# Splits of the first and last unit issued in another order, and gate weights moved behind the turned blocks

## The chip, the cores and the metric

One program runs on one core of a Trainium2 chip. TensorE (PE) multiplies matrices and loads its stationary operand separately (PEld), VectorE (DVE), ScalarE (ACT) and GpSimd (POOL) work on SBUF, and SyncE (SP) and POOL issue DMAs. Each engine takes its instructions in order; between engines semaphores hold an instruction back until what it reads is there. The metric is the device time of the program in microseconds (us). Before the change it is 651.31 us, the median of 3 runs (650.48 to 651.41).

## The reference

A decoder trunk of two layers over 256 tokens and a model width D = 1024. Layer 0 mixes tokens with forgetting attention, layer 1 with block-sparse attention; the change touches neither mixer. Behind the mixer each layer has a gated FFN and a gated per-layer input (PLE), and a final norm ends the program:

```python
u = _rmsnorm(h, ffn_norm_g[i])
gu = u @ ffn_w_in[i]
h = h + (jax.nn.silu(gu[..., :D_FF]) * gu[..., D_FF:]) @ ffn_w_out[i]
gate = jax.nn.sigmoid(_rmsnorm(h, ple_norm_g[i]) @ ple_w_gate[i])
h = h + gate * (p[i] @ ple_w_up[i])
```

`x` is 1 x 256 x 1024, `D_FF` 2816, everything float32.

## The kernel before

**Precision.** Every float32 operand is split in a rounded high part (ACT copies it into a rounded type, fp32r in the profile) and a low remainder (DVE subtracts), and every product is three PE products: high by high, high by low, low by high (lines 96, 97 and 98 of `mm3`). So weights arrive in halves of 512 KB (`half`, by SP's queue into `raw`, 6 buffers), ACT makes `whi` (L158), DVE makes `wlo` (L159), each in a ring of 6 buffers. The weight halves of a layer are numbered in the order of use; the numbers in `whi82` or `wlo169` are theirs.

**FFN.** 22 blocks f of the hidden width are computed one after the other (`gu`, `up`), two of them make a unit u = 0 to 10 (NU = 11). `gated(f)` takes a block's result from PSUM: ACT makes `sg` (L676, L677), DVE multiplies into `a32` (L685). When the second block of a unit is there, DVE makes four sums of its parts (L691 to L693), and `halves(u)` splits all seven parts into `ah` (ACT, L619) and `al` (DVE, L620). The output product is done by a scheme with seven products instead of eight, so the weights of a unit are summed too: `unit(u)` fetches them (`xr<-wu` on POOL's DMA queue; SP's for the last unit), splits the first and the fourth quarter pair, makes sums on DVE (L643, L645, L648) and splits these (`uh`, `ul`; for the last unit they live in the weight ring and are called `whiu`, `wlou`). PE then runs `fo<-uh,ah` and so on (L658). A unit's products stand between later blocks' `gu` products (`visit`). The products of the last two units come after the last block, in an order written out by hand (`last`), and their accumulators are added to the residual h (L746).

**The turn to the PLE.** `Norm.turn` transposes a half of h on PE (`tp`, L212, four blocks per half), and `Norm.block` scales and splits it into `g` (ACT L202, DVE L203). The gate's first two weight halves are not split the usual way. `summed` fetches the half with rounding as `hi` through POOL's queue (L186), ACT writes its negative into `lo` (L187), and a second DMA of POOL adds the exact weights onto that (L188). The call for both of them stands behind the rounding of the last unit's last activations.

**PLE.** `ple` computes the gate in two halves of the width. The first half `pg_0` uses the two `summed` halves and two ordinary ones; after two weight halves the second half of h is turned (`nm.turn(1)`), squares (L226) give the norm's scale on DVE (L234, L235) and POOL (`col`, L237), and ACT loads the table for the sigmoid (L108). `gate` then applies sigmoid (ACT, `pgt`, L801), the product with the input (DVE, L802) and the addition to h (DVE, L803). The second half `pg_1` takes four more weight halves: 82 to 85 in layer 0, 168 to 171 in layer 1. In layer 0 the next layer's norm turns its first blocks among them; in layer 1 the second token half is computed last and in two narrow parts (`pg_1_1` and `pgl`, 256 wide), so that the final norm's work on ACT and DVE (`sqf`, `msf`, `end`, L837 to L890) lies beside PE.

**What sets the order.** The program is traced in Python, and a scheduler places instructions on each engine by its own estimate of when they can run. Three hints bind it: `tc.issue_after(x)` keeps what is inside behind x in its engine's order, `tc.keep_in_program_order` fixes the order as traced, and tile pools make a new tile wait for the last reader of the tile whose buffer it takes. `nm.behind()` is `issue_after` both instructions of the norm's last turned block.

Of the kernel before, what the change touches and what calls it, by code (L numbers as in the profile page):

```python
# [30 lines left out]
ALU = mybir.AluOpType  # L31

P = 128
# [42 lines left out]
def trunk(ctx: ExitStack, tc: tile.TileContext, x, xg, wx, xr, pt, w, wu, cst, gf, rel, hot, rvm, out):  # L76
# [12 lines left out]
    def f32(ap):  # L89
        return ap.bitcast(F32)  # L90
# [90 lines left out]
    def summed():  # L181

        i = state["next"]
        state["next"] += 1
        hi, lo = (work.tile([P, HW + 2 * LINE], F32R, tag=n, bufs=6, name=f"{n}{i}")[:, 0:HW] for n in ("whi", "wlo"))
        nc.gpsimd.dma_start(hi, w[i - 2][:, 0:HW])  # L186
        nc.scalar.activation(lo, f32(hi), AF.Copy, scale=-1.0)  # L187
        nc.gpsimd.dma_start(lo, w[i - 2][:, 0:HW], accum_op=ALU.add)  # L188
        return hi, lo
# [421 lines left out]
    def ffn(layer, nm):  # L611
# [4 lines left out]
        left, right = {}, {}  # L616
# [5 lines left out]
        def unit(u):  # L622
# [9 lines left out]
            def pair(n, wide=HW):  # L632
                if u == NU - 1 and n != 3:
# [3 lines left out]
                        for t in ("uh", "ul")]  # L637

            p0 = pair(0)
            splits(*p0, r1[:, 0:HW])  # L640
            p3 = pair(3, HC)
            splits(*p3, r2[:, HC:HW])
            nc.vector.tensor_tensor(xs[:, 0:2], r2[:, 0:HC].unsqueeze(1).to_broadcast([P, 2, HC]),  # L643
                                    r1[:, 0:HW].rearrange("p (a c) -> p a c", c=HC), op=ALU.add)
            nc.vector.tensor_tensor(xs[:, 2], xs[:, 0], r1[:, HC:HW], op=ALU.add)  # L645
            p1 = pair(1)
            splits(*p1, xs[:, 0:2].rearrange("p a c -> p (a c)"))
            nc.vector.tensor_tensor(xs[:, 3], xs[:, 2], r2[:, HC:HW], op=ALU.add)  # L648
            p2 = pair(2)
            splits(*p2, xs[:, 2:4].rearrange("p a c -> p (a c)"))  # L650
# [22 lines left out]
        def gated(f, bk):  # L673
# [8 lines left out]
            if f % 2 == 0 and u:  # L682
                with tc.issue_after(empty.ins):
                    halves(u - 1)
# [8 lines left out]
            nc.vector.tensor_tensor(a[:, 6], a[:, 1], a[:, 5], op=ALU.add)  # L693
            if u == NU - 1:
                halves(u, (3, 7))

# [8 lines left out]
        def up(fs):  # L705
# [17 lines left out]
            for f in fs:  # L723
                gated(f, bks[f])
# [9 lines left out]
        for u in (NU - 2, NU - 1):  # L734
            unit(u)
        rounded, split = left["end"]
        with tc.issue_after(rounded.ins):
            gate = [summed(), summed()]
# [57 lines left out]
    def ple(layer, nm, ut, nx, early):  # L796
# [19 lines left out]
        if layer == 0:  # L816
            for c in range(4):
                pair_unit(bks[1], c, half(), nm.k)
                if c == 2:
                    nx.turn(0)  # L820
                    nx.square(0)
            for t in range(2):
                gate(bks[1][t], t, HC, D)
            return
# [19 lines left out]
        wts = [half(AHEAD) for _ in range(4)]  # L844
# [164 lines left out]
```

## Time and profile before

| | us |
|---|---|
| median of 3 runs | 651.31 |
| profiled execution, its own time | 649.11 |
| span of that execution's profile | 647.3 |
| PE busy | 636.0 (98%) |
| DVE busy | 522.3 (81%) |
| ACT busy | 420.6 (65%) |

The granted TensorE clock was 0.998 over the span. The profile's rows give the start of an instruction, its length, the engine, the line, the operation and the tiles as out<-in, and in brackets the engine's idle time before it with what ended it. Instructions of one line that follow each other closely stand in one row (x2). PE's rows overlap, since products are pipelined; what tells of a wait there is the step from one start to the next.

### The profile page before, as it was taken

The numbers are of one execution on the slowest core, as the hardware profiler recorded it, in microseconds if no ns is written. First come the engines' busy times: TensorE is split into PE (matmuls) and PEld (weight loads), VectorE is DVE, ScalarE is ACT, GpSimd is POOL, SyncE is SP. The second block draws the span as 40 slices with busy tenths as digits, with TensorE's granted clock in tenths as the row PEclk, the third lists the DMA queues.
The fourth block names the chain that finished last, engine by engine and source line by source line (L and its number), as shares of the span: only waits on it lengthen the run. The fifth ranks groups of instructions, "written<-read, shape, count | busy, mean of one in ns | idle before, by whom it ended". The sixth has DMA issues, their size and how long they took to land.

```text
span 647.3 us, 11656 instructions
## 1 busy us (share of the span) xinstructions
PE 636.0 (98%) x4514; PEld 578.6 (89%) x4514; DVE 522.3 (81%) x824; ACT 420.6 (65%) x725; POOL 41.1 (6%) x75
## 2 busy tenths in 40 slices
PE   9999999999999999999999999999999999999995
PEld 7899987999999999997889999789999999999774
DVE  5778884779998888878875787658898888887886
ACT  6866774976666666547866677757666666665483
POOL 1000000200000000001100000010000000000111
PEclk9999999999999999999999999999999999999999
DMA  8978544568766666534896554445677666662711
GB/s 336 376 244 282 190 128 155 166 199 286 246 199 199 199 201 205 187 121 102 277 330 207 175 173 136 133 142 186 204 266 224 226 212 200 194 214 87 174 22 65
DMA packets 36599, 127.31 MB, mean 197 GB/s; under 512 B 3968, under 2 KB 6336, under 8 KB 36544
## 3 DMA queue, kind: packets, MB, share of 16 engines
q1 hardware_dynamic: 29216, 101.00, 47.5%
q0 software_dynamic: 6912, 25.17, 13.3%
q8 instruction: 35, 0.57, 0.3%
q10 hardware_dynamic: 416, 0.40, 0.2%
q14 instruction: 20, 0.16, 0.1%
HBM read 125.48 MB, written 4.22 MB: 200 GB/s over the span
## 4 chain that ended last, share of the span: by engine, by line
PE 87%; DMA 4%; issue 3%; DVE 2%; ACT 1%; POOL 1%; POOLq 0%; ACTq 0%; DVEq 0%
PE fo L658 15%; PE gu L97 11%; PE gu L96 10%; PE gu L98 10%; PE pq L96 5%; PE pq L97 5%; PE pq L98 5%; DMA xr<-wu 3%; PE wo L96 2%; PE wo L98 2%; PE wo L97 2%; PE v L98 2%; PE v L96 2%; PE v L97 2%; PE pg L96 2%
## 5 line engine op out<-in xcount | busy, mean ns | idle before, releaser
L96 PE MATMUL gu<-g,whi 128*128 128x256 f32 x704 | 195.1, 277 | 0.0
L98 PE MATMUL gu<-g,wlo 128*128 128x256 f32 x704 | 195.0, 277 | 0.0
L97 PE MATMUL gu<-g,whi 128*128 128x256 f32 x704 | 195.0, 277 | 0.0
L159 DVE TENSOR_TENSOR wlo<-raw,whi 128x1024 fp32r<-128x1024 f32 (+1 forms) x119 | 143.6, 1213 | 45.1 <-ACT whi L158 43.4
L158 ACT ACTIVATE whi<-raw 128x1024 fp32r<-128x1024 f32 (+1 forms) x118 | 122.9, 1055 | 79.4 <-PE gu L97 37.2
L97 PEld LDWEIGHTS gu<-g,whi 128*128 128x128 f32 x704 | 132.2, 188 | 1.6
L96 PEld LDWEIGHTS gu<-g,whi 128*128 128x128 f32 x704 | 132.2, 188 | 1.4
L98 PEld LDWEIGHTS gu<-g,wlo 128*128 128x128 f32 x704 | 132.3, 188 | 0.2 <-DVE wlo L159 0.2
L175 ACT ACTIVATE whi<-raw 128x1080 fp32r<-128x1080 f32 x47 | 52.0, 1107 | 56.9 <-PE gu L97 47.3
L620 DVE TENSOR_TENSOR ul<-xr,uh 128x1024 fp32r<-128x1024 f32 (+1 forms) x80 | 85.8, 1088 | 1.9 <-ACT uh L619 1.9
L619 ACT ACTIVATE uh<-xr 128x1024 fp32r<-128x1024 f32 (+1 forms) x80 | 73.4, 953 | 10.6 <-DMA xr<-wu 9.1
L176 DVE TENSOR_TENSOR wlo<-raw,whi 128x1080 fp32r<-128x1080 f32 x47 | 60.2, 1281 | 14.5 <-ACT whi L175 14.5
L96 PE MATMUL pq<-g,whi 128*128 128x256 f32 x256 | 71.7, 280 | 0.0
L97 PE MATMUL pq<-g,whi 128*128 128x256 f32 x256 | 71.0, 277 | 0.0
L98 PE MATMUL pq<-g,wlo 128*128 128x256 f32 x256 | 71.0, 277 | 0.0
L658 PE MATMUL fo<-uh,al 128*128 128x512 f32 x142 | 55.7, 392 | 0.5 <-DVE al L620 0.5
L658 PE MATMUL fo<-uh,ah 128*128 128x512 f32 x142 | 55.7, 393 | 0.0
L658 PE MATMUL fo<-ul,ah 128*128 128x512 f32 x142 | 55.5, 391 | 0.0
L96 PEld LDWEIGHTS pq<-g,whi 128*128 128x128 f32 x256 | 48.3, 189 | 1.1 <-issue 0.6
L97 PEld LDWEIGHTS pq<-g,whi 128*128 128x128 f32 x256 | 48.1, 188 | 0.0
L98 PEld LDWEIGHTS pq<-g,wlo 128*128 128x128 f32 x256 | 48.1, 188 | 0.0
L630 POOL DMA_DIRECT2D xr<-wu x40 | 21.7, 543 | 263.5 <-DVE ul L620 195.3
(196 smaller groups left out, 1097.3 us busy)
## 6 DMA issues: line engine op xcount, KB each, us to landing
raw<-w SPq DMA_DIRECT2D x118, 512.0 KB, 4.6
raw<-w SPq DMA_DIRECT2D x47, 540.0 KB, 4.5
xr<-wu POOLq DMA_DIRECT2D x40, 512.0 KB, 5.9
d<-d SPq DMA_DIRECT2D x4, 768.0 KB, 9.4
ru<-wu SPq DMA_DIRECT2D x4, 512.0 KB, 5.2
whi<-w POOLq DMA_DIRECT2D x4, 512.0 KB, 3.7
wlo<-w POOLq DMA_DIRECT2D x4, 512.0 KB, 6.4
bias<-d SPq DMA_DIRECT2D x4, 512.0 KB, 5.4
```

Source lines behind the costliest of these rows:

```text
L96: mm(o, ah, bh, start=start, stop=False, skip_group_check=True)
L97: mm(o, ah, bl, start=False, stop=False, skip_group_check=True)
L98: mm(o, al, bh, start=False, stop=stop, skip_group_check=True)
L158: nc.scalar.activation(hi[:, c], raw[:, c], AF.Copy)
L159: nc.vector.tensor_tensor(lo[:, c], raw[:, c], f32(hi[:, c]), op=ALU.subtract)
L175: nc.scalar.activation(ht, raw[:, 0:WW], AF.Copy)
L176: nc.vector.tensor_tensor(lt, raw[:, 0:WW], f32(ht), op=ALU.subtract)
L619: first = nc.scalar.activation(hi, src, AF.Copy)
L620: return first, nc.vector.tensor_tensor(lo, src, f32(hi), op=ALU.subtract)
L630: queue.dma_start(r, wu[layer * NU + u][:, i * HW:(i + 1) * HW])
L658: got = mm(acc[i], a[x][:, SLOT[i]], b[y], start=u == 0 and n == 0, stop=u == NU - 1 and n == 2, skip_group_check=True)
```

## The change

It has four parts. No instruction is added and none is taken away: PE, ACT, POOL and SP have as many rows as before.

1. `halves(0)` and `halves(9)` are called as soon as the unit's sums are there, where before they stood behind ACT's work on the next block; and the first sum of unit 1 (L643, now L651) must come behind unit 0's sums.
2. The weights of the last two units are traced ahead of the last block's `gated`, which must come behind the last unit's low splits; in the last unit the sums of `xs` come ahead of the splits of these sums.
3. `summed` returns a second function that does the negation and the adding DMA. Both gate halves take their buffers inside the last `unit`, ahead of its pairs 1 and 2; the first half's negation is traced there too, the second half's behind the split of pair 1.
4. In `ple` the first weight half of `pg_1` comes behind the norm's last turned block.

```diff
--- before.py
+++ after.py
@@ -184,9 +184,12 @@
         state["next"] += 1
         hi, lo = (work.tile([P, HW + 2 * LINE], F32R, tag=n, bufs=6, name=f"{n}{i}")[:, 0:HW] for n in ("whi", "wlo"))
         nc.gpsimd.dma_start(hi, w[i - 2][:, 0:HW])
-        nc.scalar.activation(lo, f32(hi), AF.Copy, scale=-1.0)
-        nc.gpsimd.dma_start(lo, w[i - 2][:, 0:HW], accum_op=ALU.add)
-        return hi, lo
+
+        def end():
+            nc.scalar.activation(lo, f32(hi), AF.Copy, scale=-1.0)
+            nc.gpsimd.dma_start(lo, w[i - 2][:, 0:HW], accum_op=ALU.add)
+
+        return (hi, lo), end
 
     class Norm:
 
@@ -613,7 +616,7 @@
         xs, ru1, ru2 = (xr8[:, i:j] for i, j in ((0, 4), (4, 6), (6, 8)))
         ru1, ru2 = (r.rearrange("p a c -> p (a c)") for r in (ru1, ru2))
         np_ = Norm(3 * layer + 2)
-        left, right = {}, {}
+        left, right, gate = {}, {}, []
 
         def splits(hi, lo, src):
             first = nc.scalar.activation(hi, src, AF.Copy)
@@ -638,16 +641,29 @@
 
             p0 = pair(0)
             splits(*p0, r1[:, 0:HW])
+            if u == NU - 1:
+                (g0, first), (g1, second) = (summed() for _ in range(2))
+                gate.extend((g0, g1))
+                first()
             p3 = pair(3, HC)
             splits(*p3, r2[:, HC:HW])
-            nc.vector.tensor_tensor(xs[:, 0:2], r2[:, 0:HC].unsqueeze(1).to_broadcast([P, 2, HC]),
-                                    r1[:, 0:HW].rearrange("p (a c) -> p a c", c=HC), op=ALU.add)
+            with tc.issue_after(left["sums"].ins) if u == 1 else ExitStack():
+                nc.vector.tensor_tensor(xs[:, 0:2], r2[:, 0:HC].unsqueeze(1).to_broadcast([P, 2, HC]),
+                                        r1[:, 0:HW].rearrange("p (a c) -> p a c", c=HC), op=ALU.add)
             nc.vector.tensor_tensor(xs[:, 2], xs[:, 0], r1[:, HC:HW], op=ALU.add)
             p1 = pair(1)
-            splits(*p1, xs[:, 0:2].rearrange("p a c -> p (a c)"))
-            nc.vector.tensor_tensor(xs[:, 3], xs[:, 2], r2[:, HC:HW], op=ALU.add)
+            if u < NU - 1:
+                splits(*p1, xs[:, 0:2].rearrange("p a c -> p (a c)"))
+            last = nc.vector.tensor_tensor(xs[:, 3], xs[:, 2], r2[:, HC:HW], op=ALU.add)
+            if u == NU - 1:
+                with tc.issue_after(last.ins):
+                    got = splits(*p1, xs[:, 0:2].rearrange("p a c -> p (a c)"))
+                with tc.issue_after(got[0].ins):
+                    second()
             p2 = pair(2)
-            splits(*p2, xs[:, 2:4].rearrange("p a c -> p (a c)"))
+            got = splits(*p2, xs[:, 2:4].rearrange("p a c -> p (a c)"))
+            if u == NU - 1:
+                left["lo"] = got
             cut = lambda p, i: [t[:, i * HC:(i + 1) * HC] for t in p]
             right[u] = {1: cut(p0, 0), 3: cut(p0, 1), 2: p3, 5: cut(p1, 0), 7: cut(p1, 1), 6: cut(p2, 0), 4: cut(p2, 1)}
 
@@ -679,7 +695,7 @@
                 state32[u] = stage.tile([P, 8, P], F32, tag="a32", bufs=1, name=f"a32_{layer}_{u}")
             a = state32[u]
             o = a[:, 1:3] if f % 2 else a[:, 0:8:7]
-            if f % 2 == 0 and u:
+            if f % 2 == 0 and 1 < u < NU - 1:
                 with tc.issue_after(empty.ins):
                     halves(u - 1)
             nc.vector.tensor_tensor(o, sg[:, 0].rearrange("p (t s) -> p t s", s=P),
@@ -690,9 +706,13 @@
                 halves(u, (0, 3))
             nc.vector.tensor_tensor(a[:, 3:5], a[:, 7:8].to_broadcast([P, 2, P]), a[:, 0:3:2], op=ALU.subtract)
             nc.vector.tensor_tensor(a[:, 5], a[:, 4], a[:, 0], op=ALU.subtract)
-            nc.vector.tensor_tensor(a[:, 6], a[:, 1], a[:, 5], op=ALU.add)
+            got = nc.vector.tensor_tensor(a[:, 6], a[:, 1], a[:, 5], op=ALU.add)
             if u == NU - 1:
                 halves(u, (3, 7))
+            if u == 0:
+                left["sums"] = got
+            if u in (0, NU - 2):
+                halves(u)
 
         def halves(u, part=(0, 7)):
 
@@ -720,8 +740,14 @@
                     wt = blocks() if a else gapped()
                     for k in range(KT):
                         step(fs[0], a, wt, k, k == 0)
-            for f in fs:
-                gated(f, bks[f])
+            if fs[0] == FT - 1:
+                for u in (NU - 2, NU - 1):
+                    unit(u)
+            with ExitStack() as late:
+                for i in left.get("lo", ()):
+                    late.enter_context(tc.issue_after(i.ins))
+                for f in fs:
+                    gated(f, bks[f])
 
         up([0, 1])
         with nm.behind():
@@ -731,11 +757,7 @@
         for f in range(4, FT):
             visit((f - 4) // 2, f % 2)
             up([f])
-        for u in (NU - 2, NU - 1):
-            unit(u)
-        rounded, split = left["end"]
-        with tc.issue_after(rounded.ins):
-            gate = [summed(), summed()]
+        split = left["end"][1]
         def last(u, *which):
             for i in which:
                 for n in range(3):
@@ -815,7 +837,9 @@
             gate(bks[0][t], t, 0, HC)
         if layer == 0:
             for c in range(4):
-                pair_unit(bks[1], c, half(), nm.k)
+                with ExitStack() if c else nm.behind():
+                    wt = half()
+                pair_unit(bks[1], c, wt, nm.k)
                 if c == 2:
                     nx.turn(0)
                     nx.square(0)
@@ -841,7 +865,9 @@
             square(t, 0, 0, HC)
             nc.vector.tensor_scalar(ms[:, t, 0:1], ss[:, t, 0:1], EPS, None, op0=ALU.add)
             nc.vector.tensor_tensor(ys[:, t, 0:HC], h[:, t, 0:HC], gb[:, 0:HC], op=ALU.mult)
-        wts = [half(AHEAD) for _ in range(4)]
+        with nm.behind():
+            wts = [half(AHEAD)]
+        wts += [half(AHEAD) for _ in range(3)]
 
         def part(t, i, bk):
             c0 = HC + i * S
```

On DVE in layer 0's first unit (`a32_0_0` holds unit 0's parts, `xr0` the weights of the units), before:

```order
L685 TENSOR_TENSOR a32_0_0_1653<-sg0_1_1655 128x256
L691 TENSOR_TENSOR a32_0_0_1653<-a32_0_0_1653 128x256
L643 TENSOR_TENSOR xr0_1525<-xr0_1525 128x1024
L692 TENSOR_TENSOR a32_0_0_1653<-a32_0_0_1653 128x128
L159 TENSOR_TENSOR wlo41_1765<-raw41_1763,whi41_1764 128x1024
L693 TENSOR_TENSOR a32_0_0_1653<-a32_0_0_1653 128x128
L620 TENSOR_TENSOR ul2_0_0_1825<-xr0_1525,uh2_0_0_1824 128x1024
L176 TENSOR_TENSOR wlo42_1842<-raw42_1840,whi42_1841 128x1080
L620 TENSOR_TENSOR al0_0_1728<-a32_0_0_1653,ah0_0_1727 128x896
```

and now:

```order
L701 TENSOR_TENSOR a32_0_0_1653<-sg0_1_1655 128x256
L707 TENSOR_TENSOR a32_0_0_1653<-a32_0_0_1653 128x256
L708 TENSOR_TENSOR a32_0_0_1653<-a32_0_0_1653 128x128
L159 TENSOR_TENSOR wlo41_1765<-raw41_1763,whi41_1764 128x1024
L709 TENSOR_TENSOR a32_0_0_1653<-a32_0_0_1653 128x128
L623 TENSOR_TENSOR ul2_0_0_1825<-xr0_1525,uh2_0_0_1824 128x1024
L176 TENSOR_TENSOR wlo42_1842<-raw42_1840,whi42_1841 128x1080
L623 TENSOR_TENSOR al0_0_1663<-a32_0_0_1653,ah0_0_1662 128x896
L159 TENSOR_TENSOR wlo43_1872<-raw43_1870,whi43_1871 128x1024
```

The sum of `xr0` has left the place between unit 0's third and last sums (it stands behind `ul3_0_1` now, further down), so all that follows moves up one row.

On ACT at the end of layer 0's FFN (`ah0_9` and `ah0_10` are the last two units' activations, `wlo78` and `wlo79` the negations for the gate halves), before:

```order
L619 ACTIVATE uh3_0_10_3462<-ru0_1_3455 128x512
L676 ACTIVATE sg0_20_3340<-gu0_20_3279 128x256
L677 ACTIVATE sg0_20_3340<-gu0_20_3279 128x256
L619 ACTIVATE ah0_9_3344<-a32_0_9_3163 128x896
L619 ACTIVATE uh1_0_9_3445<-xr0_1525 128x1024
L619 ACTIVATE uh2_0_9_3450<-xr0_1525 128x1024
L619 ACTIVATE whiu0_1_3468<-xr0_1525 128x1024
L619 ACTIVATE whiu0_2_3473<-xr0_1525 128x1024
L676 ACTIVATE sg0_21_3420<-gu0_21_3359 128x256
L677 ACTIVATE sg0_21_3420<-gu0_21_3359 128x256
L619 ACTIVATE ah0_10_3424<-a32_0_10_3343 128x384
L619 ACTIVATE ah0_10_3424<-a32_0_10_3343 128x512
```

and now:

```order
L622 ACTIVATE uh3_0_10_3457<-ru0_1_3442 128x512
L189 ACTIVATE wlo78_3450<-whi78_3449 128x1024
L622 ACTIVATE ah0_9_3247<-a32_0_9_3163 128x896
L692 ACTIVATE sg0_20_3344<-gu0_20_3283 128x256
L693 ACTIVATE sg0_20_3344<-gu0_20_3283 128x256
L622 ACTIVATE uh1_0_9_3432<-xr0_1525 128x1024
L622 ACTIVATE uh2_0_9_3437<-xr0_1525 128x1024
L622 ACTIVATE whiu0_1_3463<-xr0_1525 128x1024
L189 ACTIVATE wlo79_3453<-whi79_3452 128x1024
L622 ACTIVATE whiu0_2_3470<-xr0_1525 128x1024
L692 ACTIVATE sg0_21_3474<-gu0_21_3359 128x256
L693 ACTIVATE sg0_21_3474<-gu0_21_3359 128x256
```

`ah0_9` stands ahead of the two `sg0_20`, and the negations, which came behind the rows shown before, stand ahead of `ah0_9` and between `whiu0_1` and `whiu0_2`. On POOL the four DMAs of the gate halves go hi, lo, hi, lo, where they went hi, hi, lo, lo; the first now waits for the products of block 19 to free its buffer (before: block 20), the third for the first half of block 20 (before: block 21).

On DVE in layer 1's PLE (`g5` is the turned h, `ms5` its mean square, `wlo168` to `wlo171` the low parts for `pg_1`), before:

```order
L203 SCALAR_TENSOR_TENSOR g5_5111<-tp5_2_7185,gx_87,g5_5111 128x256
L203 SCALAR_TENSOR_TENSOR g5_5111<-tp5_3_7194,gx_87,g5_5111 128x256
L159 TENSOR_TENSOR wlo169_7272<-raw169_7270,whi169_7271 128x1024
L234 TENSOR_TENSOR ms5_7213<-ss5_5112 128x2
L159 TENSOR_TENSOR wlo170_7278<-raw170_7276,whi170_7277 128x1024
L235 TENSOR_SCALAR ms5_7213<-ms5_7213 128x2
L159 TENSOR_TENSOR wlo171_7284<-raw171_7282,whi171_7283 128x1024
L802 TENSOR_TENSOR pgt1_0_0_7243<-pgt1_0_0_7243,uh1_4985 128x512
L802 TENSOR_TENSOR pgt1_1_0_7247<-pgt1_1_0_7247,uh1_4985 128x512
L803 TENSOR_TENSOR h_86<-h_86,pgt1_0_0_7243 128x512
L803 TENSOR_TENSOR h_86<-h_86,pgt1_1_0_7247 128x512
```

and now:

```order
L206 SCALAR_TENSOR_TENSOR g5_5111<-tp5_3_7194,gx_87,g5_5111 128x256
L237 TENSOR_TENSOR ms5_7213<-ss5_5112 128x2
L238 TENSOR_SCALAR ms5_7213<-ms5_7213 128x2
L159 TENSOR_TENSOR wlo168_7266<-raw168_7264,whi168_7265 128x1024
L824 TENSOR_TENSOR pgt1_0_0_7243<-pgt1_0_0_7243,uh1_4985 128x512
L824 TENSOR_TENSOR pgt1_1_0_7247<-pgt1_1_0_7247,uh1_4985 128x512
L825 TENSOR_TENSOR h_86<-h_86,pgt1_0_0_7243 128x512
L825 TENSOR_TENSOR h_86<-h_86,pgt1_1_0_7247 128x512
L867 TENSOR_TENSOR end_7251<-h_86,end_7251 128x512 x2
L866 TENSOR_SCALAR msf_7254<-ssf_7253 128x1
L159 TENSOR_TENSOR wlo169_7272<-raw169_7270,whi169_7271 128x1024
```

Before, all four low parts stood ahead of the first `pgt` product; now only `wlo168` does, and `wlo169` comes behind two `pgt`, two additions to h, two products of the final norm and one `msf`. ACT follows the same pattern: `whi168`, the table load, two `pgt`, then `whi169` and `whi170`, two `sqf`, `whi171`. Layer 0 has the same order without the final norm's rows.

PE takes its products in the order in which the scheduler expects their operands. In layer 1 behind the last product of `pg1_0`, before:

```order
L98 MATMUL pg1_1_0_7165<-whi168_7265,g5_5111 128x512
L96 MATMUL pg1_1_0_7165<-whi168_7265,g5_5111 128x512
L97 MATMUL pg1_1_0_7165<-wlo168_7266,g5_5111 128x512
L98 MATMUL pg1_1_0_7165<-whi168_7265,g5_5111 128x512
L96 MATMUL pg1_1_0_7165<-whi169_7271,g5_5111 128x512
L97 MATMUL pg1_1_0_7165<-wlo169_7272,g5_5111 128x512
L98 MATMUL pg1_1_0_7165<-whi169_7271,g5_5111 128x512
```

and now, six wide products and three narrow ones further on:

```order
L96 MATMUL pg1_1_1_7166<-whi168_7265,g5_5111 128x256
L97 MATMUL pg1_1_1_7166<-wlo168_7266,g5_5111 128x256
L98 MATMUL pg1_1_1_7166<-whi168_7265,g5_5111 128x256
L96 MATMUL pgl_7329<-whi168_7265,g5_5111 128x256
L96 MATMUL pg1_1_0_7165<-whi169_7271,g5_5111 128x512
L96 MATMUL pg1_1_1_7166<-whi169_7271,g5_5111 128x256
L97 MATMUL pgl_7329<-wlo168_7266,g5_5111 128x256
L98 MATMUL pgl_7329<-whi168_7265,g5_5111 128x256
L96 MATMUL pgl_7329<-whi168_7265,g5_5111 128x256
L97 MATMUL pgl_7329<-wlo168_7266,g5_5111 128x256
L98 MATMUL pgl_7329<-whi168_7265,g5_5111 128x256
L96 MATMUL pgl_7329<-whi169_7271,g5_5111 128x256
```

Before, wide products of `pg1_1_0` follow each other up to its end, and the narrow ones come behind; four of the products with `whi168` and `wlo168` stood further up among those of `pg1_0`. Now none of these is up there, and 14 narrow products (`pg1_1_1`, `pgl`) stand ahead of the first that reads `wlo169`. In layer 0 14 products of `pg0_1` come ahead of the first that reads `wlo83`, and the eight transposes of the next norm's first half stand between, where they stood behind the third weight half before.

## The prediction

> **What bounds the kernel now.** The page comes first: its line on engines, then the chain that ended last.
>
> ```profile
> PE 636.0 (98%) x4514; PEld 578.6 (89%) x4514; DVE 522.3 (81%) x824; ACT 420.6 (65%) x725; POOL 41.1 (6%) x75
> ...
> PE 87%; DMA 4%; issue 3%; DVE 2%; ACT 1%; POOL 1%; POOLq 0%; ACTq 0%; DVEq 0%
> ```
>
> PE is busy for 98% of the span and carries 87% of the chain, and the change leaves its instructions as they are. So only PE's waits can be won or lost. I looked for them in the timeline of PE at the places the change touches, as the step from one product's start to the next against the undisturbed step: 290.20 to 290.66 below is two steps, 0.23 us for a 512-wide product (0.2275 over longer rows; a 256-wide one steps by half, 0.1134).
>
> **FFN start (part 1).** PE in layer 0, DVE in layer 0, then PE in layer 1:
>
> ```profile
> 145.45 0.40 PE L658 MATMUL fo<-ul,ah 128*128 128x512 f32 x1
> 146.06 0.50 PE L658 MATMUL fo<-uh,al 128*128 128x512 f32 x1 [0.21 <-DVE al L620]
> ```
> ```profile
> 137.33 0.43 DVE L691 TENSOR_TENSOR a<-a 128x256 f32<-128x256 f32 x1
> 139.91 1.22 DVE L643 TENSOR_TENSOR xr<-xr 128x1024 f32<-128x1024 f32 x1 [2.15 <-DMA xr<-wu]
> ```
> ```profile
> 457.47 0.28 PE L97 MATMUL gu<-g,whi 128*128 128x256 f32 x1
> 457.76 0.39 PE L98 MATMUL gu<-g,wlo 128*128 128x256 f32 x1
> ...
> 460.60 0.40 PE L658 MATMUL fo<-ul,ah 128*128 128x512 f32 x1
> 461.29 0.50 PE L658 MATMUL fo<-uh,al 128*128 128x512 f32 x1 [0.29 <-DVE al L620]
> ```
>
> The first activations' low half (al_0) is late because unit 1's first sum of xr stands ahead of a_0's last sums on DVE and waits 2.15 us for its DMA. Its move behind those sums takes 2.15 + 1.1 us out of the chain. Counted again without it: a's third sum at 137.8, wlo41 to 139.2, the last sum to 139.5, ul2 to 140.6, wlo42 to 141.8, al_0 to 142.9, against 145.7 when PE wants it. PE's step of 0.61 shrinks to 0.23, and the product behind a wait steps by 0.34 instead of 0.23 (619.31 to 619.65 below), so layer 0 gains 0.38 + 0.11 = **0.49**. In layer 1 the same wait holds a weight split too: 0.18 + 0.11 at 457.76 and 0.46 + 0.11 at 461.29, **0.86** in all. The moved sum is 1.1 us more for what stands behind it there, unit 1's splits:
>
> ```profile
> 159.39 1.22 DVE L620 TENSOR_TENSOR ul<-xr,uh 128x1024 fp32r<-128x1024 f32 x1
> ```
> ```profile
> 163.55 0.39 PE L658 MATMUL fo<-uh,ah 128*128 128x512 f32 x1
> ```
>
> The split of that sum ends at 160.6, and PE's first product with it starts at 163.55: 2.9 us cover the 1.1.
>
> **FFN end (parts 1 to 3).** PE around the last pair's first products, layers 0 and 1; DVE's last split; the first turned blocks:
>
> ```profile
> 290.20 0.39 PE L658 MATMUL fo<-uh,ah 128*128 128x512 f32 x1
> ...
> 290.66 0.39 PE L658 MATMUL fo<-uh,al 128*128 128x512 f32 x1
> ...
> 293.69 0.39 PE L658 MATMUL fo<-whiu,ah 128*128 128x512 f32 x1
> ```
> ```profile
> 605.87 0.39 PE L658 MATMUL fo<-uh,al 128*128 128x512 f32 x1
> ...
> 608.90 0.40 PE L658 MATMUL fo<-whiu,ah 128*128 128x512 f32 x1
> ```
> ```profile
> 292.60 0.69 DVE L620 TENSOR_TENSOR al<-a,ah 128x512 fp32r<-128x512 f32 x1 [0.70 <-ACT ah L619]
> ```
> ```profile
> 297.80 1.22 PE L212 MATMUL tp<-con,h 128*128 128x128 f32 x8
> ...
> 613.00 1.24 PE L212 MATMUL tp<-con,h 128*128 128x128 f32 x8
> ```
>
> From 290.66 to 293.69 PE takes ten steps in 3.03 us, where 2.28 would do: 0.75, and again 0.75 in layer 1. The eight transposes behind lose another 0.2 in each, waiting for h. All of it hangs on the last pair's split of a_10, last of a chain on ACT and DVE. The change lets ah_9 run ahead of sg_20 instead of behind it and puts the sum of xr at L651 ahead of ul2_9; against that, one negation (1 us) now stands between whiu_1 and whiu_2. What holds the chain then is uh1_9, whose buffer PE frees some four products after the gate pair that sg_20 reads, so it gains only about 0.7: the split of 292.60 ends at 292.6 instead of 293.3. PE wants it in the product ahead of 293.69, at 293.35 in this trace and, 0.75 earlier, at 292.6. There is no margin, so I leave 0.1 in layer 0: **0.85** and **0.95**. If the chain gains nothing all of it stays (second rival).
>
> **Gate halves (part 3).** Layer 0, then layer 1:
>
> ```profile
> 299.15 0.50 PE L96 MATMUL pg<-whi,g 128*128 128x512 f32 x1
> ...
> 302.48 0.39 PE L98 MATMUL pg<-whi,g 128*128 128x512 f32 x1
> ```
> ```profile
> 614.37 0.50 PE L96 MATMUL pg<-whi,g 128*128 128x512 f32 x1
> ...
> 619.31 0.50 PE L97 MATMUL pg<-wlo,g 128*128 128x512 f32 x1 [1.30 <-DMA wlo<-w]
> 619.65 0.40 PE L98 MATMUL pg<-whi,g 128*128 128x512 f32 x1
> ```
>
> From the first gate product to the fifteenth layer 1 takes 5.28 us where layer 0, in the same order, takes 3.33. The difference, **1.95**, is waits for the low parts that DMAs add up. With the negations some 6 to 15 us earlier, and POOL issuing hi, lo, hi, lo instead of hi, hi, lo, lo, both are there in time. Layer 0 gains nothing here.
>
> **The weights behind the turned blocks (part 4).** This part costs. ACT now does the four g, two squares, whi82, the table load and both pgt before whi83; DVE splits wlo83 only behind pgt and h. Layer 0 on PE, ACT, DVE and POOL; then layer 1's POOL and DVE:
>
> ```profile
> 307.25 0.40 PE L98 MATMUL pg<-whi,g 128*128 128x512 f32 x1
> ...
> 307.99 0.39 PE L97 MATMUL pg<-wlo,g 128*128 128x512 f32 x1
> ```
> ```profile
> 306.19 1.06 ACT L158 ACTIVATE whi<-raw 128x1024 fp32r<-128x1024 f32 x1
> ...
> 311.10 1.28 ACT L108 ACT_TABLE_LOAD   x1
> ...
> 314.16 1.25 ACT L801 ACTIVATE pgt<-pg,col 128x512 f32<-128x512 f32 x2
> ```
> ```profile
> 303.63 2.35 DVE L159 TENSOR_TENSOR wlo<-raw,whi 128x1024 fp32r<-128x1024 f32 x2
> ...
> 311.08 2.35 DVE L159 TENSOR_TENSOR wlo<-raw,whi 128x1024 fp32r<-128x1024 f32 x2
> 314.86 1.29 DVE L802 TENSOR_TENSOR pgt<-pgt,uh 128x512 f32<-128x512 f32 x2 [1.43 <-ACT pgt L801]
> ```
> ```profile
> 311.26 2.75 POOL L237 TENSOR_TENSOR col<-ms,nhalf 128x2 f32<-128x2 f32 x1 [15.63 <-DVE ms L235]
> ```
> ```profile
> 628.00 1.62 POOL L237 TENSOR_TENSOR col<-ms,nhalf 128x2 f32<-128x2 f32 x1 [17.16 <-DVE ms L235]
> ```
> ```profile
> 627.81 1.23 DVE L159 TENSOR_TENSOR wlo<-raw,whi 128x1024 fp32r<-128x1024 f32 x1
> ```
>
> On layer 0's clock, with the first turned block at 297.80 as before: DVE ends two splits at 305.98, its four g take to 307.8, ACT's fourth g ends at 307.35, two squares (0.6 each) at 308.55, whi82 at 309.6, the table load at 310.9. col starts at 308.9 and ends before that if it takes the 0.58 that it took in both layers once the split beside it was done (313.43 and 629.04 to its ends). pgt runs from 311.1 to 312.4, whi83 to 313.4; DVE's pgt and h (1.25 each pair) end at 314.25, wlo83 at 315.45. PE has its last 24 gate products of the first half from 305.64 (0.2275 each, 0.1 lost on g) to 311.2; then 14 products and the eight turned blocks (0.87), which came last before, to 315.25. So layer 0 waits about 0.25 here; the old wait for g, 0.74 - 0.455 = 0.29 from 307.25 to 307.99, shrinks to 0.1. Together **0**.
>
> Layer 1 has no turned blocks there, and DVE puts two further products (ys, 1.29) and msf ahead of wlo169: ready at 316.85. PE's cover is 7 products of 512 and 14 of 256, 3.18 us: done at 314.4. **Stall 2.45 us.** Moreover the 14 narrow ones were the tail's cover, 12 of them net, 1.36 us. The last of 17 wide products then starts at 316.85 + 16 x 0.2275 = 320.5, 22.7 us after the first turned block, where it was 20.9 (613.00 to 633.90). With the turned block 0.95 earlier it comes **0.85 later** than before. The tail:
>
> ```profile
> 633.90 0.39 PE L98 MATMUL pg<-whi,g 128*128 128x512 f32 x1
> ```
> ```profile
> 639.24 0.28 PE L98 MATMUL pgl<-whi,g 128*128 128x256 f32 x1
> ```
> ```profile
> 640.12 0.43 DVE L802 TENSOR_TENSOR pgt<-pgt,uh 128x256 f32<-128x256 f32 x1 [0.16 <-ACT pgt L801]
> ```
>
> PE's own last product moves to about 638.75, 0.5 earlier. But the chain through ACT and DVE that begins at 633.90 has only 0.16 us of slack at 640.12, so the end moves by 0.85 - 0.16, about **+0.7** within layer 1 behind its FFN start.
>
> **Sum**: -0.49 - 0.85 + 0 - 0.86 + 0.7 = -1.5 against the profiled execution's 649.11, so 647.6. That execution lies 2.2 us under the median of 651.31, and I take the difference over to it: 649.8.
>
> [...] In both rows col ends 0.58 us after the split beside it, so it seems to wait for that split. [...]
>
> **Rivals.** First, **no stall**: the chain on ACT and DVE turns out some 2 us shorter. Then only the 1.36 us of lost cover is paid: the last wide product moves by 0.85 - 2.45 = -1.6, the tail with it instead of by +0.7, and the time is 649.8 - 2.2 = 647.6. Against it stands that DVE's order is fixed and every link has a row. Chance 0.14.
>
> Second, **the last pair is late anyway**: no margin against seven links. The 0.85 and 0.95 stay: 651.6. Chance 0.16.
>
> Third, **col meets wlo82**, whose split starts 0.75 after col may: col then ends 0.58 behind it, 0.35 to 0.75 more in each layer, 650.9. Chance 0.10.
>
> Fourth, the one that ends **slower: PE's clock falls in layer 1's stall**. The first products of the kernel came behind an idle PE at half speed:
>
> ```profile
> 0.78 4.61 PE L115 MATMUL cold<-const-float32-0.0 128*128 128x512 f32 x10 [0.78 <-PEq L1001]
> ```
>
> They step by 0.46. If 2.45 us of idle were enough, ten products behind it at 0.23 more would cost 2.3: 652.1, more if it lasts. The gap before 619.31 was not enough, since 0.34 follows it and then 0.23. Chance 0.05. [...]
>
> **How the numbers follow.** The forecast has 0.55, with 648.8 to 650.8 as its own range. Differences under 0.2%, 1.3 us, can't be told from no change here: the limits are 650.0 and 652.6. The forecast lies just inside the first of them: 0.34 faster, 0.21 the same. Rival one adds 0.14 to faster; two 0.11 to same and 0.05 to slower; three 0.08 and 0.02; four 0.05 to slower. Faster 0.48, same 0.40, slower 0.12. The range runs from the first rival's 647.6, half of which lies below, to 652.0, above the second and just below the fourth.
>
> **What would show it.** In the new profile: no DVE wait at the sum of xr (L651) in front of al_0; ten steps of 0.23 at the last pair; no wait of pg for a DMA; col near 0.6; in layer 1 one PE wait for wlo at pg of about 2.4, and in layer 0 one under 0.5; and at the end PE finishing early while DVE's products wait in a row. I am wrong if that stall is under 1 or above 3.3 us, or if the last pair still waits for al.

## The result, and the profile after

The changed kernel takes 648.26 us, the median of nine runs (646.45 to 649.37), against 651.31 for the kernel before, measured beside it in nine runs of its own (648.32 to 653.68): a ratio of 0.9947, with a 95% interval of 0.9926 to 0.9968. The profiled execution took 646.60, 2.5 less than the one of before. One execution among all that follow, of the changed kernel, ran at a clearly lower granted clock (657.92 us at 0.944) and is left out of every comparison.

First the two lines of its page that answer to those of before, the engines and the chain that ended last.

```profile
PE 632.5 (98%) x4514; PEld 577.5 (90%) x4514; DVE 522.5 (81%) x824; ACT 422.0 (65%) x725; POOL 39.1 (6%) x75
...
PE 95%; DVE 2%; ACT 2%; issue 1%; POOL 0%; POOLq 0%; ACTq 0%; DVEq 0%
```

PE's share of the chain has gone from 87 to 95%, and the 4% of DMA in it are gone. The timeline of PE at the places of the prediction: the two FFN starts, the last pairs (the same ten steps as before), and layer 1's gate from its first to its fifteenth product.

```profile
145.36 0.40 PE L674 MATMUL fo<-ul,ah 128*128 128x512 f32 x1
145.59 0.39 PE L674 MATMUL fo<-uh,al 128*128 128x512 f32 x1
...
290.05 0.39 PE L674 MATMUL fo<-uh,al 128*128 128x512 f32 x1
...
292.43 0.40 PE L674 MATMUL fo<-whiu,ah 128*128 128x512 f32 x1
...
458.02 0.40 PE L674 MATMUL fo<-ul,ah 128*128 128x512 f32 x1
458.26 0.39 PE L674 MATMUL fo<-uh,al 128*128 128x512 f32 x1
...
602.71 0.39 PE L674 MATMUL fo<-uh,al 128*128 128x512 f32 x1
...
605.09 0.40 PE L674 MATMUL fo<-whiu,ah 128*128 128x512 f32 x1
...
610.40 0.50 PE L96 MATMUL pg<-whi,g 128*128 128x512 f32 x1
...
613.73 0.39 PE L98 MATMUL pg<-whi,g 128*128 128x512 f32 x1
```

The step in front of al is 0.23 and 0.24 (before, 0.61 and 0.69). Ten steps of the last pair take 2.38 in both layers (3.03). The fifteen gate products take 3.33 (5.28). All three waits went as foreseen. Then the place where the change costs: PE, DVE and ACT in layer 1's second half of the gate.

```profile
625.53 0.28 PE L96 MATMUL pgl<-whi,g 128*128 128x256 f32 x1
627.78 0.50 PE L97 MATMUL pg<-wlo,g 128*128 128x512 f32 x1 [1.97 <-DVE wlo L159]
...
631.62 0.39 PE L98 MATMUL pg<-whi,g 128*128 128x512 f32 x1
```
```profile
624.04 1.29 DVE L825 TENSOR_TENSOR h<-h,pgt 128x512 f32<-128x512 f32 x2
625.25 1.28 DVE L867 TENSOR_TENSOR end<-h,end 128x512 f32<-128x512 f32 x2
...
626.51 1.21 DVE L159 TENSOR_TENSOR wlo<-raw,whi 128x1024 fp32r<-128x1024 f32 x1
...
637.59 0.42 DVE L824 TENSOR_TENSOR pgt<-pgt,uh 128x256 f32<-128x256 f32 x1
```

PE waits 1.97 us for wlo169, whose split stands behind pgt, h and the two products of the final norm (`end`, called ys in the prediction). The last wide product starts at 631.62, and at the end DVE's last pgt has no idle time before it: from the last wide product on the tail runs through ACT and DVE, no longer through PE's narrow products. From the fifteenth gate product to the end the changed kernel gives back 3.4 of the 5.9 us by which PE was early at 613.73. In POOL's timeline col takes 0.72 in both layers, where it took 2.75 and 1.62:

```profile
307.57 0.72 POOL L240 TENSOR_TENSOR col<-ms,nhalf 128x2 f32<-128x2 f32 x1 [20.51 <-DVE ms L238]
...
620.24 0.72 POOL L240 TENSOR_TENSOR col<-ms,nhalf 128x2 f32<-128x2 f32 x1 [20.52 <-DVE ms L238]
```

Two things did not fit. The medians differ by 3.05 us where the terms gave 1.5, and the nine times lie in two groups, 646.45 to 646.91 and 648.26 to 649.37, with nothing between.

### The profile page after: what moved, and what is told of

Its sections match the earlier page's. It is cut to its first block, busy times and chain, and to the rows that moved or that the text cites. A ratio compares the mean times of both kernels' runs of the same rounds, so it can differ in the third digit from the quotient of the medians.

```text
span 644.8 us, 11655 instructions
## 1 busy us (share of the span) xinstructions
PE 632.5 (98%) x4514; PEld 577.5 (90%) x4514; DVE 522.5 (81%) x824; ACT 422.0 (65%) x725; POOL 39.1 (6%) x75
## 4 chain that ended last, share of the span: by engine, by line
PE 95%; DVE 2%; ACT 2%; issue 1%; POOL 0%; POOLq 0%; ACTq 0%; DVEq 0%
PE fo L674 16%; PE gu L97 12%; PE gu L98 12%; PE gu L96 12%; PE pq L96 5%; PE pq L98 5%; PE pq L97 5%; PE wo L96 2%; PE wo L98 2%; PE wo L97 2%; PE v L97 2%; PE v L98 2%; PE v L96 2%; PE pg L97 1%; PE pg L96 1%; PE pg L98 1%
```

## The experiments

**What part 4 costs, and where.** Parts 1 to 3 without part 4; the same with part 4 in layer 0 alone; and part 4 alone, put into the kernel before. Here is the edit of the second, against the changed kernel; the first takes back layer 0's lines of part 4 as well, and the third puts both places into the kernel before.

```diff
-        with nm.behind():
-            wts = [half(AHEAD)]
-        wts += [half(AHEAD) for _ in range(3)]
+        wts = [half(AHEAD) for _ in range(4)]
```

> Parts 1 to 3 without part 4. Theory: part 4 costs about 2 us in layer 1. Without it PE's wait of 2.0 us for wlo169 is gone, the narrow products are back at the end, and from the first turned block of layer 1 to the end of the last DVE product it takes about 28.6 us instead of 30.8. Layer 0 loses about 0.15. Time about 2 us under the changed kernel, ratio to the kernel before about 0.992. Rival: part 4 pays for itself, because without it col, held up by the splits beside it, and the old waits for g delay the tail by as much: the time stays within 0.5 us of the changed kernel, ratio 0.995. col is expected back at 1.6 us or more in both layers, 0.7 with part 4.

> Parts 1 to 3, and part 4 in layer 0 alone. Theory: as without part 4, and 0.1 to 0.2 us faster than that from layer 0, too little to be told in the times but to be seen in PE's starts behind layer 0's PLE; ratio to the kernel before about 0.992. Rival (part 4 is neutral in both layers): 0.995.

> Part 4 alone on the kernel before. Theory: layer 1's PE waits 2.0 us for wlo169 on top of its 2.0 us for the gate halves, and the tail's chain starts later: from the first turned block to the end 32.8 us instead of 29.6, time about 654, ratio 1.005. Rival: the late gate halves cover the late weights, so the stall is under 0.5 us and the time 651 to 652, ratio 1.000 to 1.001.

Measured: 643.39 us (643.18 to 643.83), ratio 0.9899 [0.9859, 0.9939]; 643.51 (643.38 to 643.59), ratio 0.9899 [0.9863, 0.9935]; and 653.12 (650.41 to 654.83), ratio 1.0046 [1.0020, 1.0073]. Layer 0 has no part in the cost: the two times differ by no more than their spread, and on PE's timeline part 4 wins 0.1 us there (0.35 behind parts 1 to 3 at layer 0's first turned block, 296.52 against 296.17, and 0.26 at layer 1's, 609.15 against 608.89). All of the cost is in layer 1; part 4 alone makes the kernel before slower, with a wait of 1.92 us at the same product. By the profiles (643.18 and 646.60) it costs 3.4 us, by the medians nearly 5. Leaving it out makes the best version measured here, 1.0% below the kernel before. Without part 4 POOL's timeline has the old col again, beside DVE's splits:

```profile
309.45 2.76 POOL L240 TENSOR_TENSOR col<-ms,nhalf 128x2 f32<-128x2 f32 x1 [22.75 <-DVE ms L238]
...
622.18 1.62 POOL L240 TENSOR_TENSOR col<-ms,nhalf 128x2 f32<-128x2 f32 x1 [22.78 <-DVE ms L238]
```

Also to be explained now: these two kernels spread by 0.65 and 0.2 us, the kernel before, measured beside them, by 9 (645.92 to 655.15).

**The sum of xr: left ahead, and moved alone.** The changed kernel without the hint on unit 1's first sum; the kernel before with that hint and nothing else; and the kernel before profiled again. The edit of the second:

```diff
+            with tc.issue_after(left["sums"].ins) if u == 1 else ExitStack():
                 nc.vector.tensor_tensor(xs[:, 0:2], ...
```

> The change without the one hint that keeps unit 1's first sum behind unit 0's sums. Theory: that sum's wait for its DMA is the whole cause at the start of the FFN, so PE's waits there are back, 0.6 us in layer 0 and 0.8 in layer 1, 1.4 us in all over the changed kernel, and DVE again waits over 2 us at the sum. Rival: the earlier rounding of the first activations (ah_0 ahead of sg_2) is what helps: then under 0.3 us are lost.

> The kernel before with one thing changed: unit 1's first sum of xr stands behind a_0's last sums on DVE (the second half of part 1's first edit), and everything else as before. The profiles of kernels that keep the sum ahead show it waiting 2.15, 2.21 and 2.73 us for its transfer in layer 0 and 2.42, 2.71 and 4.82 in layer 1, and their times spread over 5 to 9 us. If that wait is the main source of the spread, the FFN-start waits of PE are gone here, the lowest times change little, and the long ones go: all executions between 645 and 649.5, median about 647.5, ratio 0.994 to 0.997; what is left of the spread are the gate halves' low parts, which wait from 0 to 2 us by the landing of their transfers. If the spread comes from elsewhere, the ratio is 0.998 (the 1.35 us that the profile of the kernel before shows) and the times still spread over 6 us or more.

> The kernel before, one more profiled execution, to see which of its waits are the same from run to run. Those of the last pair hang on ACT's and DVE's order alone: ten steps in 3.0 us again in both layers. Those that end with a transfer differ: the sum of xr in layer 0 and 1 (2.15 and 2.42 us in the first profile) and the gate halves' low part in layer 1 (1.30) may be anything from 0 to 5.

Without the move the changed kernel takes 652.07 (650.59 to 657.03), ratio 1.0026 [0.9997, 1.0055]: 3.8 more than with it, not 1.4. The move alone takes the kernel before to 645.65 (645.21 to 646.05), ratio 0.992 [0.9897, 0.9943]: 5.2 us, more than the whole change. DVE's timelines show why the first profile had it too small. The sum in front of al_0 in layer 0 and 1, first in the second profile of the kernel before (649.47 us), then in layer 1 of the changed kernel without the move and of part 4 alone:

```profile
140.65 1.22 DVE L643 TENSOR_TENSOR xr<-xr 128x1024 f32<-128x1024 f32 x1 [2.60 <-DMA xr<-wu]
...
457.19 1.22 DVE L643 TENSOR_TENSOR xr<-xr 128x1024 f32<-128x1024 f32 x1 [4.50 <-DMA xr<-wu]
```
```profile
456.34 1.23 DVE L651 TENSOR_TENSOR xr<-xr 128x1024 f32<-128x1024 f32 x1 [4.82 <-DMA xr<-wu]
```
```profile
455.03 1.23 DVE L643 TENSOR_TENSOR xr<-xr 128x1024 f32<-128x1024 f32 x1 [2.71 <-DMA xr<-wu]
```

In layer 1 the wait was 2.4, 2.7, 4.5 and 4.8 us in four profiles. POOL issues the transfer at 449.1 to 449.8 in all four; the sum starts 5.3, 5.8, 7.3 and 7.4 us later. Behind the sum stands a weight split, and PE waits for that. In the first profile of the kernel before the step in front of the product that needs it is 0.29 (457.47 to 457.76 in the prediction's rows), where 0.11 is a step; in the second profile it is 2.40, and PE is idle for most of it:

```profile
459.81 0.39 PE L98 MATMUL gu<-g,wlo 128*128 128x256 f32 x1 [2.12 <-DVE wlo L159]
```

With the sum moved no transfer ends any idle time of DVE there, in either layer, and the spread falls to 0.84 us. From the second profile of the kernel before to that of the moved sum, PE gains 4.3 us, 3.0 of them at layer 1's FFN start.

**The gate's low parts.** Parts 1 and 2 alone, with both gate halves summed late as before.

```diff
-            if u == NU - 1:
-                (g0, first), (g1, second) = (summed() for _ in range(2))
-                ...
+        with tc.issue_after(rounded.ins):
+            for _ in range(2):
+                both, end = summed()
+                gate.append(both)
+                end()
```

> Parts 1 and 2 alone: the gate halves are summed late, as in the kernel before, and the weights behind the turned blocks come as before. Against parts 1 to 3 (643.4, ratio 0.990) layer 1's gate waits come back: 1.95 to 2.0 us, so 645.4 and a ratio of 0.993. Clock theory: the longest single wait there is 1.45 us, and all waits within 3.4 us add up to no more than 1.6, too little to halve the clock, so the times stay within 1 us; if they spread over 2 us or more, waits of that size are enough. Transfer theory: narrow, since the sum of xr no longer waits.

Measured: 644.14 (644.01 to 645.42), ratio 0.9914 [0.9883, 0.9946]. The 1.95 us did not come back: layer 1 has no wait for a low part (its fifteen gate products take 3.32), layer 0 one of 0.33.

```profile
301.52 0.50 PE L97 MATMUL pg<-wlo,g 128*128 128x512 f32 x1 [0.33 <-DMA wlo<-w]
```

Nor is there one in part 4 alone, in the moved sum alone, or in the second profile of the kernel before, which all sum late; layer 1's fifteen products take 3.50, 3.58 and 3.38 there, where they took 5.28. The wait of 1.30 in the first profile was that execution's: there one of the four adding transfers took 9.3 us from issue to landing; in the others the slowest took 7.1 to 7.9. Against parts 1 to 3, part 3 is worth 0.5 us on PE's timeline, most of it in layer 0, and 0.75 in the medians.

**The two groups of times.** The changed kernel again; with the final norm's first products behind all four splits (wait of 0.7 expected); and with these products done twice (wait of 3.3).

```diff
-        for t in range(2):
-            square(t, 0, 0, HC)
-            nc.vector.tensor_scalar(ms[:, t, 0:1], ss[:, t, 0:1], EPS, None, op0=ALU.add)
-            nc.vector.tensor_tensor(ys[:, t, 0:HC], h[:, t, 0:HC], gb[:, 0:HC], op=ALU.mult)
         with nm.behind():
             wts = [half(AHEAD)]
         wts += [half(AHEAD) for _ in range(3)]
+        low = state["lo"]
+        for t in range(2):
+            square(t, 0, 0, HC)
+            with tc.issue_after(low.ins):
+                ...
```
```diff
-            nc.vector.tensor_tensor(ys[:, t, 0:HC], h[:, t, 0:HC], gb[:, 0:HC], op=ALU.mult)
+            for _ in range(2):
+                nc.vector.tensor_tensor(ys[:, t, 0:HC], h[:, t, 0:HC], gb[:, 0:HC], op=ALU.mult)
```

> The changed kernel once more, on the chip of the three runs below. So far its nine executions lay at 646.5 to 649.4, and the mean granted clock in their records was 0.996 to 0.997 in the four that took 646.5 to 647 and 0.994 in the five that took 648 to 649.4; parts 1 to 3 alone, without the stall of 2.0 us in layer 1, lay within 0.65 us. Clock theory: a PE that waits for about 2 us can find its clock halved for some 3.4 us behind the wait, by chance from run to run, at about 1.7 to 2 us each time. Then the executions come in two groups here too, near 646.6 with a clock of 0.996 and near 648.7 with 0.994, 3 to 7 in 10 in the upper one. Rival, transfer theory: only the landing time of the transfers for which the sum of xr waits differs from run to run; this kernel has no such wait, so its times lie within 1 us of each other here, and the clock does not go with them.

> The change, with the final norm's two first products (ys) and msf behind all four splits of layer 1's second half of the gate on DVE instead of ahead of the second one. If DVE's order makes the stall, wlo169 is ready 1.3 us earlier: PE waits 0.7 instead of 2.0 there, and everything behind moves by 1.3 (645.3 where the changed kernel takes 646.6). If not, the wait stays at 2.0. Clock theory: with 0.7 no execution finds its clock halved, so times within 1 us of each other, and a median 2 to 3.5 below the changed kernel's. Transfer theory: as narrow as the changed kernel, and 1.3 below it.

> The change, with each of the final norm's two first products (ys) done twice, so that 1.3 us more of DVE stand ahead of wlo169 and PE waits 3.3 us there instead of 2.0; the output is the same. Without the clock: 647.9, as narrow as the changed kernel, a step of 1.3 above it. Clock theory: most executions now find the clock halved behind the wait, 1.7 us or more each, so a median near 649.8 with the lowest at 647.9, and a mean granted clock of 0.994 or less in the long ones; the profile, if it is one of these, shows products that step by 0.46 behind the wait.

PE's waits for wlo169 in the second and the third of these kernels:

```profile
626.90 0.50 PE L97 MATMUL pg<-wlo,g 128*128 128x512 f32 x1 [0.69 <-DVE wlo L159]
```
```profile
629.35 0.50 PE L97 MATMUL pg<-wlo,g 128*128 128x512 f32 x1 [3.23 <-DVE wlo L159]
```

DVE's order sets the wait: 0.69, 1.97, 3.23. The times: the changed kernel again 646.57 to 647.20 in three executions and 647.97 to 648.77 in eight, the clock 0.997 in the three and 0.994 or 0.995 in the eight; ratio 0.996 [0.9942, 0.9979]. With the wait of 0.69: 645.52 (644.91 to 645.97), no second group, ratio 0.9929 [0.9902, 0.9957]. With 3.23: four executions at 647.66 to 648.43 with a clock of 0.996, eight at 648.99 to 650.53 with 0.992 to 0.995; median 649.43, ratio 0.9987 [0.9968, 1.0006]. The mean clock tells the groups apart only within one kernel: three of the five executions with the wait of 0.69 have 0.995 and are short. The transfer theory, by which all three would be narrow, falls. Two more profiled executions, to catch a long one:

> The changed kernel, one more profiled execution. Of its 21 executions so far about half are some 2 us longer than the others. If this one is such a one (near 648.5), the clock theory expects products that step by 0.43 to 0.46 us instead of 0.23 for up to 3.4 us behind the wait for wlo169, 1.3 to 1.7 us in all, with the granted clock at half there, and everything ahead of that wait as in the first profile; if it is not (near 646.6), no such products. A long execution without them speaks against the clock theory.

> The kernel with the wait of 3.3 us, one more profiled execution. Eight of its twelve executions lay above 648.9 and four at 647.7 to 648.4, that of its profile among them, which showed no slow products. The same readings as for the run above: near 649.5 with products that step by 0.43 to 0.46 us behind the wait, or near 648 without; a long execution without them speaks against the clock theory.

The changed kernel took 648.58 this time, and here are PE's timeline behind the wait and a table of stretches (length; PE busy, PEld, DVE, ACT, POOL; then the granted clock). The wait is put down to `msf` here, which DVE ends within 0.1 us of the split of wlo169.

```profile
628.22 0.58 PE L97 MATMUL pg<-wlo,g 128*128 128x512 f32 x1 [1.95 <-DVE msf L866]
628.60 0.63 PE L98 MATMUL pg<-whi,g 128*128 128x512 f32 x1
629.02 0.63 PE L96 MATMUL pg<-whi,g 128*128 128x512 f32 x1
...
631.15 0.63 PE L98 MATMUL pg<-whi,g 128*128 128x512 f32 x1
631.58 0.54 PE L96 MATMUL pg<-whi,g 128*128 128x512 f32 x1
631.96 0.39 PE L97 MATMUL pg<-wlo,g 128*128 128x512 f32 x1
632.19 0.39 PE L98 MATMUL pg<-whi,g 128*128 128x512 f32 x1
```
```profile
626.00:628.00 2.00, 0.26 (x3) 0.06 (x1) 2.00 (x4) 1.87 (x5) 0.00 (x0) 1.00 0.00 0
628.00:629.00 1.00, 0.78 (x2) 0.63 (x3) 1.00 (x3) 0.00 (x0) 0.00 (x0) 0.74 0.00 0
629.00:630.00 1.00, 1.00 (x4) 0.78 (x3) 1.00 (x2) 0.00 (x0) 0.00 (x0) 0.50 0.00 0
630.00:631.00 1.00, 1.00 (x4) 0.81 (x3) 0.49 (x1) 0.00 (x0) 0.00 (x0) 0.50 0.00 0
631.00:632.00 1.00, 1.00 (x4) 0.76 (x4) 0.00 (x0) 0.00 (x0) 0.00 (x0) 0.55 0.00 0
632.00:633.00 1.00, 1.00 (x6) 0.82 (x5) 0.00 (x0) 0.00 (x0) 0.00 (x0) 1.00 0.00 0
```

Behind the wait nine products step by 0.38 to 0.43 instead of 0.23. The clock is granted at half for 0.52 + 1 + 1 + 0.9 = 3.4 us. Up to the wait this execution runs 0.45 us behind the first profile, behind it 1.98: the halved clock costs 1.5. The second of them took 648.30, one of the short ones, and shows none of it, as expected. Over all executions 14 of 21 of the changed kernel are long, and 8 of 13 with the wait of 3.23: the longer wait did not make it likelier, which the clock theory had expected.

What goes with it in a given execution can be read from the traces. The times between two changes of the clock are whole multiples of 3.413 us (638.29 is 187 of them in the first profile of the kernel before, 634.88 is 186 in that of the changed kernel, 10.24 three behind the halved stretch above), so in these traces the clock changed at the ends of stretches of that length, and the first change comes at another moment in each execution (6.42 us from the span's start in the first profile of the kernel before, 4.91 in that of the changed kernel). Here is the stretch with the wait and the two behind it in the long execution; then the emptiest stretch of the first profile of the changed kernel, whose wait is cut by a boundary at 626.14; then the two that share the wait of 3.23 (PE busy, then the clock):

```profile
625.07:628.48 3.41, 1.46 (x11) 1.00 0.00 0
628.48:631.90 3.42, 3.42 (x9) 0.50 0.00 0
631.90:635.31 3.41, 3.41 (x22) 1.00 0.00 0
```
```profile
626.14:629.55 3.41, 1.77 (x8) 1.00 0.00 0
```
```profile
624.17:627.58 3.41, 1.96 (x16) 1.00 0.00 0
627.58:631.00 3.42, 1.65 (x7) 1.00 0.00 0
```

In the long execution the whole wait lies in one stretch, PE is busy for 43% of it, and the next stretch runs at half. In the others a boundary cuts the wait, PE is busy for 48% or more of each part, and the clock stays. The other traces agree: a stretch with PE busy for 42% or less, at the kernel's end, is followed by half clock (41% in part 4 alone, none at all in the first profile of the kernel before), and none with 48% or more is (48% in the stretch ahead of that one in the kernel before). This is read off the profiles and not tested by a run of its own; by it the wait of 3.23 should be hit more often than that of 1.97, which 8 of 13 against 14 of 21 do not show.

## Why the prediction was right or wrong

**The FFN starts.** Place, cause and mechanism hold. The size, 1.35, held from profile to profile (0.65 and 0.87), but not over runs: moved alone, the sum was worth 5.2 us of median. The step that failed is taking one execution's 2.15 and 2.42 us as the wait, without asking how it varies; it ends with a transfer that comes 5.3 to 7.4 us after its issue, and where the sum's wait grew from 2.42 to 4.50, PE's own step grew from 0.29 to 2.40. The spread of the shown runs, 0.93, gave no hint; more runs of the same kernel spread by 4 to 9. Taking 2.2 over from one execution to the median carried the same error.

**The last pairs.** Predicted 0.85 and 0.95; from profile to profile 0.81 in both layers, from the moved sum alone to parts 1 to 3 some 1.1 and 0.8. The size is right, with 0.1 left in each layer (2.38 for ten steps that could take 2.28). One step of it is not: the 0.2 at the transposes does not hang on the last pair. With parts 1 and 2 alone the ten steps take 2.32, and yet the gate's first product comes 1.34 and 1.33 behind the first turned block, as before (1.35 and 1.37); it comes after 1.16 and 1.17 only with part 3. Through which wait part 3 does this stays open.

**The gate halves.** 1.95 predicted, 1.95 found from profile to profile (5.28 to 3.33), and yet wrongly priced: it is a loss of that one execution, absent from the four others that sum late, so part 3 bought 0.5 to 0.75, not 1.95.

**Part 4.** In layer 0 costed at 0, measured as a gain of 0.1. In layer 1 the stall is 1.97 instead of 2.45: the chain on ACT and DVE was 0.5 shorter than I counted (the product behind it starts 18.5 after the first turned block, where I had 19.05). The last wide product came 22.4 behind the first turned block (609.24 to 631.62), for 22.7 predicted, and DVE ends the tail as described. Taken from the fifteenth gate product, my terms gave back 0.7 + 0.95 + 1.95 = 3.6, measured 3.4.

**col and the split beside it.** col takes 0.72 where no split runs as it starts (in both layers one starts 0.50 behind it), against 0.58 worked out, and 2.76 and 1.62 where one does. The third rival did not come: in layer 1 wlo168's split starts at 620.74, while col still runs until 620.96, and col is not held up.

**The fourth rival** had 0.05, my estimate, and came in 14 of 21 executions. I gave it ten products at 0.23; it is nine, 1.5 us. The mistake was to hold the unharmed step behind a wait of 1.45 against one of 2.45: a longer wait leaves PE idle for more of a stretch of 3.41 us, 57% in the long execution against 38% around 619.31. PE's longest wait in the first profile of the kernel before is 1.30; one of 1.95 was followed by 3.4 us at half clock. The other rivals did not come. Two sums among the rivals are off: from +0.7 to -1.6 the first one's tail moves by 2.3 and not 2.2, so 647.5; and the fourth's 652.1 lies under the 652.6 that I set as the limit for slower.

**The sum**, in medians: 650.9 for the kernel before, 5.2 for the sum of xr, 2.3 for what is left of parts 1 to 3 (645.65 to 643.39), 3.2 back for part 4 in short executions (643.4 to 646.6), and 1.4 to 2.8 more in the long ones, in which the median lies: 648.0 to 649.4, measured 648.26 and, in the eleven later executions, 648.08. These terms are differences of measured medians, so that they add up proves nothing by itself; each has its own run. So the time came out 1.5 below the forecast because one gain was nearly four times as large as priced, partly eaten by one that never was there (the gate's) and by a loss that I had nearly excluded. That the time lay near the forecast is therefore in good part luck: the errors, of 1 to 4 us each, ran against each other. Between the two profiles a further 0.7 went in places that no edit touches (pq and gu products of layer 1 that step by 0.118 instead of 0.113 for some 60 products at a time); other runs have it elsewhere.

What stays open: how much of the spread of the kernel before is the clock, too. A PE wait of 2.12 is longer than the 1.95 that half clock followed, but no profile caught it there: in the second profile of the kernel before the stretch with this wait has PE busy for 51%, the clock stays at 1.00, and from 460.03 on the 256-wide products behind it step by 0.11 to 0.12.

## What to carry to other kernels

A wait that ends with a transfer was not a number here but a range (2.4 to 4.8 us for the sum of xr in layer 1): look at it in several executions before pricing it, and where an engine that runs in order meets such a wait, put what doesn't need the transfer ahead of it; that alone narrowed the times from 4.4 us beside it to 0.84. A stall of PE of some 2 us can cost more than its length: behind one of 1.95 the clock was halved for 3.4 us, which cost 1.5; with the stall at 0.69 the second group of times was gone. An edit that wins time ahead of a narrow end should be tried without its companions: three parts of this change were worth 7 us, and the fourth took back 3 to 5.

## What the hardware showed that I had not expected

- PE's granted clock was halved for 3.4 us behind a wait of 1.95 us. In these traces the clock changed only at the ends of stretches of 3.413 us whose place differs from execution to execution (the first change at 6.42 and 4.91 us): it fell behind stretches in which PE was busy for 43% or less, and stayed behind those with 48% or more. With a wait of 0.69 none of five executions showed a second group of times.
- The four adding transfers of 512 KB each took 5.4 to 9.3 us from issue to landing within one execution, and in layer 1 the sum of xr, which waits for a transfer, started 5.3 to 7.4 us after the issue in four executions.
